# A list scheduler that books VectorE and GpSimd as taking turns, in one step of a hybrid decoder layer

## The chip, the cores and the metric

The kernel runs on one core of a Trainium2 chip. Its engines work side by side, each through its own list of instructions in order: PE (TensorE, matrix products), DVE (VectorE), ACT (ScalarE), POOL (GpSimd), and SP (SyncE), which issues the DMA transfers. A semaphore holds an instruction until what it reads is there. The metric is the device time of one execution in microseconds (us); a smaller number is better.

## What is computed

One inference step of one layer, for 512 new prompt tokens and 8 x 8 sample tokens with stored states: three token mixers beside each other (A is HGRN2, B is mLSTM, C is a gated delta rule, all recurrent over chunks), each branch projected to 1024 channels, merged by gates, one output projection, a LayerNorm, a SwiGLU FFN and a second LayerNorm. Everything is float32.

```python
proj = jnp.einsum('bld,dn->bln', h, w_in[l])          # all inputs of A, B, C and the merge gates
...
a = bc[..., :, None] * jnp.einsum('bhtk,bhsk->bhts', kc, kc) * _masked_exp(strict, diff)
sol = lax.linalg.triangular_solve(eye + a, rhs, left_side=True, lower=True, unit_diagonal=True)
...
z = jnp.einsum('blnc,ncd->blnd', ys, w_branch[l])
gates = jax.nn.sigmoid(mg.reshape(B, L, N_BRANCH, D_MODEL).astype(f32))
merged = jnp.sum(gates * z.astype(f32), axis=2).astype(dt)
h = _layer_norm(ALPHA * h.astype(f32) + (merged @ w_out[l]).astype(f32), ln1_g[l], ln1_b[l]).astype(dt)
gate, up = jnp.split(h @ w_ffn_in[l], 2, axis=-1)
ff = (jax.nn.silu(gate) * up) @ w_ffn_out[l]
h = _layer_norm(ALPHA * h.astype(f32) + ff.astype(f32), ln2_g[l], ln2_b[l]).astype(dt)
```

## The kernel before

Activations lie with channels on the 128 partitions and the 576 tokens in the columns, in two halves of 288. Every large product is made in three passes: `split` (line 524) parts a float32 operand into a rounded high part (a cast on ACT, `wh`, `xh`, `hh`) and a low part (a subtraction on DVE, `wl`, `xl`, `hl`), and `gemm` (line 546) adds high x high, high x low and low x high. So each weight that DMA brings (`load_w`, line 532: raw tile `wr`, then `wh` and `wl`) costs DVE one subtraction of 1024 columns before TensorE can use its low part.

All instructions are first recorded by `Plan` in the order of the program; `Plan.schedule` (line 272) then plays a model of the five engines forward and picks, at each step, the instruction that can start earliest, with ties by priority. The lists that result are the program; because one line of the file issues all of them, every row of the profile bears the number 434. [...] `FLEX` is a string of site letters: an operation recorded with such a letter (`plan.tt`, `plan.ts`, `plan.copy`, `plan.square`) may go to any of several engines, and `place` picks the one on which it is modelled to end first, with POOL's length weighted by `PSLOW`; other sites keep their first engine.

`ORDER` (line 33) is the order in which the stages are recorded: v (projection and convolution of C), p (preparation of a chunk of C), di (the inverse of the 32 x 32 diagonal blocks of C's triangular systems, `gdn_diag`, line 890), m (merging the blocks' inverses, `gdn_merge`, first product `pp`), c (the chunk steps of C, `c_step`, products `ks`, `tv`, `su`, `po`), C (sample heads of C), h (heads of A, products `pz`), a and A (chunk steps and sample heads of A, product `spo`), bq, bv, B, BS (mLSTM, result `bnt`), and X, Y, Z (the 24 merges: a projection `p` of 48 matmuls and a branch product `g` of 24). A + or - raises or lowers the priority from there on. The projections `p` depend on nothing but weights, so they are what fills TensorE while a branch waits.

`gdn_diag` is a chain on DVE: 31 times a product `dp` and an addition to `dY`, each on the result of the one before; the inverse then goes by DMA to DRAM and back into the tile `Tm`, which `pp` reads. `kk` is the product from which the blocks come. In the first LayerNorm (class `LN`, line 1543) each row block `lr` of 128 channels has a mean `m` and a factor `rstd` applied, is split into `hh` and `hl`, and goes into sums `acc`; `T` and `S` are the sums of activation and weight blocks of the FFN's first product, which has seven products `pq` in place of eight (`act_blocks`, line 1690; `weight_blocks`, line 1724). `fg` and `fu` are gate and up part of the FFN, `fh` and `fl` the split of their product.

Of the kernel before, what the change touches and what calls it, by code (L numbers as in the profile page):

```python
# [19 lines left out]
H = 4  # L20
# [11 lines left out]

ORDER = "- v20 v02 v10 + rc rb v31 v21 v32 v30 v11 v01 v00 v22 v12 p1 p2 um p3 p4 cA p0 qe cg di m2 m1 c1 m4 c2 m3 bo cs - c3 c4 C0 aA + h0 h1 h2 C1 C3 h3 a1 a2 bq a3 C2 a4 as A0 co bA A3 A2 ag A1 bv X4 ao br B1 B2 B3 Z3 Z1 B4 Z7 Z0 X0 X1 X6 BS yb ov X3 Z5 Y2 X2 Z6 Y4 X7 Y1 Z2 Y5 X5 Y0 Z4 Y3 Y6 Y7"
WALL = 100000
WDMA = 800
FLEX = "ADEFGacdhioqzIJWMNO"
WARM = 18
# [4 lines left out]
LNEXP = "natural_log_exp_and_others"  # L42
PSLOW = 1.0
LAT = {("DVE", "ACT"): 120.0, ("ACT", "DVE"): 133.0, ("POOL", "ACT"): 72.0, ("POOL", "DVE"): 72.0, ("ACT", "POOL"): 200.0,
       ("DVE", "POOL"): 180.0, ("PE", "ACT"): 215.0, ("PE", "DVE"): 215.0, ("ACT", "PE"): 160.0, ("DVE", "PE"): 145.0,
       ("POOL", "PE"): 95.0, ("PE", "POOL"): 260.0}
PORT = {(1, 3): 0.55, (1, 4): 0.15, (2, 3): 0.8, (2, 4): 0.35}
WINDOW = 3413.0


class _Op:
    __slots__ = ("eng", "fn", "a", "k", "cost", "lat", "nb", "preds", "succs", "prio", "seq",
                 "tiles", "start", "done", "npred", "ready", "alts", "lock", "act")


def _meet(a, b):
    return a[0] < b[1] and b[0] < a[1] and a[2] < b[3] and b[2] < a[3]
# [6 lines left out]
class Plan:  # L64
# [35 lines left out]
    def cost(self, eng, name, out, a, k):  # L100
        n = 1
# [13 lines left out]
        if eng == "ACT":  # L115
            return 95 + 0.834 * n + 93 * cols
        if eng == "DVE":
# [7 lines left out]
        if eng == "POOL":  # L125
            if name == "memset":
                return 66 + 0.79 * n
            if any(0 in [st for st, _ in v.ap[1:]] for v in ap_args):
                return 110 + 1.94 * n
            return (740 if name == "tensor_copy" and n < 100 else 132) + {"tensor_copy": 3.7, "tensor_scalar": 2.86}.get(  # L130
                name, 2.38) * n
        return 450.0
# [16 lines left out]
    def add(self, eng, name, fn, a, k):  # L149
        o = _Op()  # L150
# [9 lines left out]
        preds = set()  # L160
        for t, r in reads:
            preds.update(q for q, w in self.wr.get(t, ()) if _meet(r, w))
        for t, r in writes:
            for book in (self.wr, self.rd):
                lst = book.setdefault(t, [])
                preds.update(q for q, w in lst if _meet(r, w))
                book[t] = [(q, w) for q, w in lst if not _covers(r, w)]
# [13 lines left out]
        if eng == "PE":  # L181
            n = 1
# [5 lines left out]
        if eng == "SP":  # L188
            n = 4
# [7 lines left out]
    def table(self, name, after):  # L197

        o = _Op()
        o.eng, o.fn, o.a, o.k = "ACT", self.nc.scalar.preload_act_table_set, (name,), {}  # L200
        o.seq = len(self.ops)
        o.preds, o.succs, o.prio = {q.seq for q in after}, [], (-1, o.seq)
        o.cost, o.nb, o.tiles, o.alts, o.lock, o.act = 1300.0, 0, [], None, 0, 0.0
        self.ops.append(o)
        return o
# [48 lines left out]
    def schedule(self):  # L254
# [16 lines left out]
        for o in ops:  # L271
            for t in o.tiles:
                if t not in index:
                    g = self.tag[t]
# [32 lines left out]
        end = {}  # L307
        busy = {"DVE": (0.0, 0), "POOL": (0.0, 0)}
        cold, wend, wact, wide = True, 1100.0, 0.0, False
# [29 lines left out]
        while len(order) < len(ops):  # L339
# [37 lines left out]
            if o.eng == "PE":  # L377
# [10 lines left out]
                if cold:  # L388
                    took += act
                part = min(1.0, (wend - s_) / took)  # L390
                wact += act * part
                if part < 1.0:
                    cold = wact < WINDOW * (0.4 if cold else 0.385)
                    wact = act * (1.0 - part)
                    wend += WINDOW
            elif o.eng in busy:
                dve = o.eng == "DVE"
                till, lock = busy["POOL" if dve else "DVE"]
                if o.lock and lock and till > s_:
                    v, g = (o.lock, lock) if dve else (lock, o.lock)  # L400
                    kv = PORT[v, g]
                    kg = 0.33 if v == 1 else 0.2
                    both = min(till - s_, took / (1 - kv)) if dve else min((till - s_) / (1 - kv), took)
                    mine, his = (kv, kg) if dve else (kg, kv)
                    took += mine * both
                    eft["POOL" if dve else "DVE"] += his * both
                    busy["POOL" if dve else "DVE"] = (till + his * both, lock)
                busy[o.eng] = (s_ + took, o.lock)
            eft[o.eng] = s_ + took
# [11 lines left out]
            for u in o.succs:  # L421
                u.npred -= 1
                d = 250.0 if o.eng == "SP" else 0.0 if o.eng == u.eng else LAT.get((o.eng, u.eng), 150.0)
                u.ready = max(u.ready, o.done + d)
                if not u.npred:
                    place(u)
# [20 lines left out]
def tile_hybrid(ctx: ExitStack, tc: tile.TileContext, t):  # L447
# [128 lines left out]
    n = 0  # L576
# [551 lines left out]
    eblA = const.tile([P, 4, 12], F32, name="eblA")  # L1128
    akd, aqe, aatt = [], [], []
    aatt_s = sl([4, 64], name="aatts")  # L1130

    def a_head(h):
# [15 lines left out]
        at = sl([4, P], name="aatt")  # L1148
        aatt.append(at)

# [50 lines left out]
        plan.tt("D", G, q_, b_, q_, ALU.mult)  # L1201
        akd.append(k_)
        aqe.append(q_)

# [808 lines left out]
```

## Time and profile before

Three runs took 1223.35, 1223.98 and 1227.55 us.

| | before |
|---|---|
| median of the runs | 1223.98 us |
| the profiled execution's own time | 1224.88 us |
| its span, from first to last instruction | 1223.1 us |
| mean granted TensorE clock | 0.968 |
| instructions of PE, DVE, ACT, POOL on the page | 8561, 1454, 1055, 390 |

The profile is of one execution. A row of the groups view gives engine, operation, output and inputs by name (numbers left out), shapes, the count, then busy time in us and the mean of one in ns, then the engine's idle time before it and what ended that. A row of the windows view gives a stretch of the span and, for each engine, busy time and count. A row of the timeline gives start and length in us. [...]

### The profile page before, as it was taken

The page shows a single profiled execution, that of the slowest core. Times are in us where ns is not written, and L with a number is a line of the kernel's source. Part 1 is how long each engine was busy: PE and PEld are TensorE (multiplying, and loading weights), DVE is VectorE, ACT ScalarE, POOL GpSimd, SP SyncE. Part 2 cuts the span into 40 slices and gives each one's busy share as a digit, 9 for nine tenths or more (in the row PEclk, how much of TensorE's full clock was granted, in tenths as well). Part 3 has the DMA queues.
Part 4 walks back from the last instruction along what each step waited for, and adds up shares of the span by engine and source line. Part 5 has one row for each costly group of instructions (what it writes and reads, how often), then busy time and mean ns, then how long its engine had stood idle before and what let it go on. Part 6 is the DMA issues. An engine that isn't in the chain of part 4 may idle for free.

```text
span 1223.1 us, 21823 instructions
## 1 busy us (share of the span) xinstructions
PE 1169.0 (96%) x8561; PEld 1132.3 (93%) x8561; DVE 857.7 (70%) x1454; ACT 571.9 (47%) x1055; POOL 403.6 (33%) x390
## 2 busy tenths in 40 slices
PE   9999998999999999899999999959999999999996
PEld 8999987899888989899999999949999999999995
DVE  4789997599775565745644448696999989873237
ACT  6467844345443734543434453553444554432234
POOL 1177623148653553102400004642200024542223
PEclk9999999999998789999999999969999999999998
DMA  8322324311122322223222432222424342533243
GB/s 259 114 100 74 94 70 130 107 52 61 53 87 96 108 91 66 60 97 100 76 82 91 147 89 76 78 70 69 133 89 145 121 157 83 179 112 93 82 115 119
DMA packets 66910, 123.08 MB, mean 101 GB/s; under 512 B 14192, under 2 KB 28272, under 8 KB 66808
## 3 DMA queue, kind: packets, MB, share of 16 engines
q1 hardware_dynamic: 66808, 121.70, 31.3%
q8 instruction: 67, 1.10, 0.4%
q14 instruction: 35, 0.29, 0.1%
HBM read 103.37 MB, written 18.17 MB: 99 GB/s over the span
## 4 chain that ended last, share of the span: by engine, by line
PE 78%; DVE 12%; ACT 4%; issue 2%; DMA 2%; POOL 1%; SPq 0%; DVEq 0%; ACTq 0%; POOLq 0%
PE p L434 25%; PE g L434 21%; PE pq L434 17%; PE tk L434 3%; PE pz L434 2%; DVE wl L434 2%; DVE lr L434 2%; PE os L434 1%; PE spo L434 1%; PE ssu L434 1%; DVE dY L434 1%; DVE dp L434 1%; PE po L434 1%; DVE num L434 1%; DVE z L434 1%
## 5 line engine op out<-in xcount | busy, mean ns | idle before, releaser
L434 DVE TENSOR_TENSOR wl<-wr,wh 128x1024 fp32r<-128x1024 f32 (+3 forms) x172 | 187.7, 1101 | 175.5 <-PE g L434 63.8
L434 ACT CAST wh<-wr 128x1024 fp32r<-128x1024 f32 (+3 forms) x192 | 156.4, 825 | 255.2 <-PE p L434 119.1
L434 PE MATMUL p<-xh,wl 128*128 128x288 f32 x960 | 213.1, 301 | 6.5 <-DVE wl L434 6.5
L434 PE MATMUL p<-xh,wh 128*128 128x288 f32 x960 | 215.3, 302 | 3.0 <-ACT wh L434 2.1
L434 PE MATMUL p<-xl,wh 128*128 128x288 f32 x960 | 213.4, 301 | 0.0
L434 PEld LDWEIGHTS p<-xh,wl 128*128 128x128 f32 x960 | 157.4, 192 | 9.0 <-DVE wl L434 7.2
L434 PEld LDWEIGHTS p<-xh,wh 128*128 128x128 f32 x960 | 157.1, 191 | 5.5 <-ACT wh L434 2.3
L434 PEld LDWEIGHTS p<-xl,wh 128*128 128x128 f32 x960 | 156.9, 191 | 1.5 <-issue 1.1
L434 PE MATMUL g<-fh,wl 128*128 128x320 f32 (+1 forms) x352 | 82.6, 295 | 0.0
L434 PE MATMUL g<-fl,wh 128*128 128x320 f32 (+1 forms) x352 | 82.3, 295 | 0.0
L434 PE MATMUL g<-fh,wh 128*128 128x320 f32 (+1 forms) x352 | 82.3, 294 | 0.0
L434 PE MATMUL pq<-hh,wh 128*128 128x288 f32 x240 | 72.5, 302 | 8.2 <-ACT hh L434 4.1
L434 PE MATMUL pq<-hh,wl 128*128 128x288 f32 x240 | 71.7, 299 | 4.1 <-DVE wl L434 4.1
L434 PE MATMUL pq<-hl,wh 128*128 128x288 f32 x240 | 71.6, 299 | 0.6 <-DVE hl L434 0.6
L434 PE MATMUL pq<-Th,wh 128*128 128x288 f32 x240 | 70.5, 295 | 0.0
L434 PE MATMUL pq<-Tl,wh 128*128 128x288 f32 x240 | 70.5, 294 | 0.0
L434 PEld LDWEIGHTS g<-fh,wl 128*128 128x128 f32 x352 | 57.1, 188 | 0.1
L434 PEld LDWEIGHTS g<-fh,wh 128*128 128x128 f32 x352 | 57.1, 188 | 0.1
L434 PEld LDWEIGHTS g<-fl,wh 128*128 128x128 f32 x352 | 57.0, 188 | 0.0
L434 PEld LDWEIGHTS pq<-hh,wh 128*128 128x128 f32 x240 | 45.8, 191 | 9.8 <-ACT hh L434 4.5
L434 POOL TENSOR_SCALAR acc<-lr 128x288 f32<-128x288 f32 (+2 forms) x4 | 4.9, 1230 | 142.2 <-DVE lr L434 142.2
L434 PEld LDWEIGHTS pq<-hh,wl 128*128 128x128 f32 x240 | 45.9, 191 | 4.3 <-DVE wl L434 4.3
(461 smaller groups left out, 3060.9 us busy)
## 6 DMA issues: line engine op xcount, KB each, us to landing
wr<-wft SPq DMA_DIRECT2D x60, 512.0 KB, 3.5
wr<-wfi SPq DMA_DIRECT2D x20, 512.0 KB, 3.6
wq<-wfi SPq DMA_DIRECT2D x40, 256.0 KB, 3.2
wr<-wfo SPq DMA_DIRECT2D x20, 512.0 KB, 3.5
wr<-wbr SPq DMA_DIRECT2D x24, 256.0 KB, 2.6
fd<-fg SPq DMA_DIRECT2D x20, 288.0 KB, 2.3
fx<-fd SPq DMA_DIRECT2D x20, 288.0 KB, 4.0
wr<-wfo SPq DMA_DIRECT2D x10, 384.0 KB, 3.1
```

Source lines behind the costliest of these rows:

```text
L434: o.fn(*o.a, **o.k)
```

## The change

The table `PORT` goes. In its place an operation with a lock waits, in the model, until the other engine's locked operation has ended (less a lag). Costs of POOL's operations are set anew, a delay is booked between two operations of one engine where the second reads the first's result, and the cold clock multiplies a matmul's length. `PSLOW` goes from 1 to 3, `FLEX` opens other sites (among them m, i, j, n, M, A, C, and no longer a to e or z), and `ORDER` is a new one. The last hunks only index three lists by the head, since the heads are now recorded in the order 2, 0, 3, 1.

```diff
-ORDER = "- v20 v02 v10 + rc rb v31 v21 v32 v30 v11 v01 v00 v22 v12 p1 p2 um p3 p4 cA p0 qe cg di m2 m1 c1 m4 c2 m3 bo cs - c3 c4 C0 aA + h0 h1 h2 C1 C3 h3 a1 a2 bq a3 C2 a4 as A0 co bA A3 A2 ag A1 bv X4 ao br B1 B2 B3 Z3 Z1 B4 Z7 Z0 X0 X1 X6 BS yb ov X3 Z5 Y2 X2 Z6 Y4 X7 Y1 Z2 Y5 X5 Y0 Z4 Y3 Y6 Y7"
+ORDER = "- cA rc v31 v20 v11 v30 + v01 v22 um rb v21 v00 v10 v02 v32 v12 p3 p1 p4 p2 p0 qe di m1 m2 c1 aA cs c2 m3 c3 m4 c4 cg C0 - + bo h2 ov C1 h0 bA h3 C3 h1 bq a1 a2 a3 C2 a4 co br as A0 A3 ag A2 A1 bv ao B1 Z1 Z0 B2 X6 X0 Z3 Z5 B3 B4 X3 BS X1 Z7 X7 yb Y2 Y5 Y0 X5 X2 Z6 Y3 X4 Z2 Y4 Y1 Z4 Y6 Y7"
...
-FLEX = "ADEFGacdhioqzIJWMNO"
+FLEX = "DWNOgCnhwjtpqsGmrFBoMAfxidK"
...
-PSLOW = 1.0
+PSLOW = 3.0
 LAT = {("DVE", "ACT"): 120.0, ("ACT", "DVE"): 133.0, ("POOL", "ACT"): 72.0, ("POOL", "DVE"): 72.0, ("ACT", "POOL"): 200.0,
        ("DVE", "POOL"): 180.0, ("PE", "ACT"): 215.0, ("PE", "DVE"): 215.0, ("ACT", "PE"): 160.0, ("DVE", "PE"): 145.0,
-       ("POOL", "PE"): 95.0, ("PE", "POOL"): 260.0}
-PORT = {(1, 3): 0.55, (1, 4): 0.15, (2, 3): 0.8, (2, 4): 0.35}
+       ("POOL", "PE"): 95.0, ("PE", "POOL"): 260.0, ("PE", "PE"): 0.0, ("DVE", "DVE"): 121.0,
+       ("ACT", "ACT"): 131.0, ("POOL", "POOL"): 40.0}
...
-            return 95 + 0.834 * n + 93 * cols
+            return (70 if isinstance(k.get("bias"), bass.AP) else 95) + 0.834 * n + 93 * cols
...
-                return 66 + 0.79 * n
+                return 60 + 0.72 * n
+            if name == "tensor_copy":
+                return 148 + 0.8 * n if n < 100 else 120 + 3.36 * n
+            if name == "tensor_scalar":
+                return 120 + 2.6 * n
             if any(0 in [st for st, _ in v.ap[1:]] for v in ap_args):
-                return 110 + 1.94 * n
-            return (740 if name == "tensor_copy" and n < 100 else 132) + {"tensor_copy": 3.7, "tensor_scalar": 2.86}.get(
-                name, 2.38) * n
+                return 126 + 1.76 * n
+            return 146 + 2.16 * n
...
+        o.raw = set(preds)
...
-        busy = {"DVE": (0.0, 0), "POOL": (0.0, 0)}
+        held = {"DVE": 0.0, "POOL": 0.0}
...
                 if cold:
-                    took += act
+                    took *= 1.92 if o.act < 0 else 1.82
...
-            elif o.eng in busy:
-                dve = o.eng == "DVE"
-                till, lock = busy["POOL" if dve else "DVE"]
-                if o.lock and lock and till > s_:
-                    v, g = (o.lock, lock) if dve else (lock, o.lock)
-                    kv = PORT[v, g]
-                    kg = 0.33 if v == 1 else 0.2
-                    both = min(till - s_, took / (1 - kv)) if dve else min((till - s_) / (1 - kv), took)
-                    mine, his = (kv, kg) if dve else (kg, kv)
-                    took += mine * both
-                    eft["POOL" if dve else "DVE"] += his * both
-                    busy["POOL" if dve else "DVE"] = (till + his * both, lock)
-                busy[o.eng] = (s_ + took, o.lock)
+            elif o.lock:
+                other, lag = ("POOL", 99.0) if o.eng == "DVE" else ("DVE", 43.0)
+                took += max(0.0, held[other] - lag - s_)
+                held[o.eng] = s_ + took
+                if o.fn.__name__ == "tensor_scalar" and o.eng == "POOL":
+                    held[o.eng] -= max(0.0, 0.71 * o.cost - 105.0)
...
-                d = 250.0 if o.eng == "SP" else 0.0 if o.eng == u.eng else LAT.get((o.eng, u.eng), 150.0)
+                d = LAT.get((o.eng, u.eng), 250.0 if o.eng == "SP" else 150.0)
+                if o.eng == u.eng != "SP" and o.seq not in u.raw:
+                    d = 0.0
...
-    akd, aqe, aatt = [], [], []
+    akd, aqe, aatt = [None] * H, [None] * H, [None] * H
...
-        aatt.append(at)
+        aatt[h] = at
...
-        akd.append(k_)
-        aqe.append(q_)
+        akd[h] = k_
+        aqe[h] = q_
```

The instructions are the same work on other engines and in another order: DVE has 1648 in place of 1456, POOL 205 in place of 395, ACT 1037 in place of 1039; PE has 8011 and SP 376 as before. Three places:

DVE in the chain of `dp` and `dY` (dX and dY are the blocks and their inverses, `wl` a weight's low part, `so` a decayed state of a sample head, `ge` a gate), before:

```order
L434 TENSOR_TENSOR dp_467<-dX_450,dY_451 64x256
L434 TENSOR_TENSOR dY_451<-dY_451,dp_467 64x16x16
L434 TENSOR_TENSOR dp_468<-dX_450,dY_451 64x255
L434 TENSOR_TENSOR dY_451<-dY_451,dp_468 64x15x17
L434 TENSOR_TENSOR wl_555<-wr_553,wh_554 128x1024
L434 TENSOR_TENSOR dp_469<-dX_450,dY_451 64x252
L434 TENSOR_TENSOR dY_451<-dY_451,dp_469 64x14x18
L434 TENSOR_TENSOR dp_470<-dX_450,dY_451 64x247
L434 TENSOR_TENSOR dY_451<-dY_451,dp_470 64x13x19
L434 TENSOR_TENSOR dp_471<-dX_450,dY_451 64x240
L434 TENSOR_TENSOR dY_451<-dY_451,dp_471 64x12x20
L434 TENSOR_TENSOR dp_472<-dX_450,dY_451 64x231
```

and at the same products with the change:

```order
L434 TENSOR_TENSOR dp_434<-dX_422,dY_423 64x231
L434 COPY dX_455<-dY_456 32x8x8
L434 TENSOR_TENSOR dY_423<-dY_423,dp_434 64x21x11
L434 TENSOR_TENSOR dp_435<-dX_422,dY_423 64x240
L434 TENSOR_TENSOR so_574<-ss_563,eblC 128x512
L434 TENSOR_TENSOR wl_577<-wr_575,wh_576 128x1024
L434 TENSOR_TENSOR dY_423<-dY_423,dp_435 64x20x12
L434 TENSOR_TENSOR wl_583<-wr_581,wh_582 128x1024
L434 TENSOR_TENSOR dp_436<-dX_422,dY_423 64x247
L434 TENSOR_SCALAR ge_559<-ge_559 128x576
L434 TENSOR_TENSOR dY_423<-dY_423,dp_436 64x19x13
```

The chain's steps now have weight splits, a gate and the decay of sample states between them more often; the decays were POOL's.

POOL in the first LayerNorm (`lr` are the row blocks, `acc` the running sums, `T` the sums of activation blocks, `S` and `wq` those of weights), before:

```order
L434 TENSOR_TENSOR acc_1267_1376<-acc_1267_1376,lr_1467 128x288
L434 TENSOR_TENSOR acc_1268_1377<-acc_1268_1377,lsq_1494 128x288
L434 TENSOR_TENSOR acc_1268_1377<-acc_1268_1377,lsq_1496 128x288
L434 TENSOR_TENSOR acc_1267_1376<-acc_1267_1376,lr_1476 128x288
L434 TENSOR_TENSOR acc_1268_1377<-acc_1268_1377,lsq_1498 128x288
L434 TENSOR_TENSOR S_1479_1588<-wq_1582,wq_1584 128x512
L434 TENSOR_TENSOR wq_1584<-wq_1584,wq_1585 128x512
L434 TENSOR_TENSOR S_1500_1609<-wr_1605,wr_1606 128x512
L434 TENSOR_TENSOR lr_1423<-lr_1423,rstd_1379 128x288
L434 TENSOR_TENSOR lr_1441<-lr_1441,rstd_1379 128x288
L434 TENSOR_TENSOR lr_1476<-lr_1476,rstd_1379 128x288
L434 TENSOR_TENSOR lr_1476<-lr_1476,m_1271_1380 128x288
```

and with the change:

```order
L434 TENSOR_TENSOR acc_1267_1376<-acc_1267_1376,lr_1458 128x288
L434 TENSOR_TENSOR hl_1394<-lr_1467,hh_1386 128x288
L434 TENSOR_TENSOR acc_1267_1376<-acc_1267_1376,lr_1467 128x288
L434 TENSOR_TENSOR acc_1267_1376<-acc_1267_1376,lr_1476 128x288
L434 TENSOR_TENSOR lr_1448<-lr_1448,rstd_1379 128x288
L434 TENSOR_TENSOR lr_1476<-lr_1476,rstd_1379 128x288
L434 TENSOR_TENSOR lr_1476<-lr_1476,m_1271_1380 128x288
L434 TENSOR_TENSOR hl_1395<-lr_1476,hh_1387 128x288
L434 TENSOR_TENSOR T_1440_1549<-lr_1476,lr_1441 128x288
L434 TENSOR_TENSOR T_1428_1537<-lr_1458,lr_1423 128x288
L434 TENSOR_TENSOR T_1434_1543<-lr_1467,lr_1434 128x288
L434 TENSOR_TENSOR T_1446_1555<-lr_1485,lr_1448 128x288
```

The sums of squares (`lsq`) and weight blocks have gone to DVE, and of the row blocks some; two splits (`hl`) have come.

PE in the steps of the gated delta rule (`qp`, `qt`, `pp` belong to the merging, `su`, `po`, `ks` to a step, `ssu` to a sample head, `p` is a projection; x4 stands for four such rows in succession), before:

```order
L434 MATMUL qp_536<-pm_535,Tm_533 64x64 x4
L434 MATMUL p_602<-xh_98,wh_600 128x288
L434 MATMUL p_602<-xl_106,wh_600 128x288 x2
L434 MATMUL p_602<-xh_98,wl_601 128x288 x2
L434 MATMUL qt_537<-Tm_533,pm_535 128x128 x3
L434 MATMUL ssu_590<-vm_589,kh_419 128x512
L434 MATMUL ssu_590<-vm_589,kl_420 128x512
L434 MATMUL qt_537<-Tm_533,pm_535 128x128
L434 MATMUL p_602<-xh_99,wh_600 128x288
L434 MATMUL ssu_593<-vm_592,kh_419 128x512
L434 MATMUL ssu_593<-vm_592,kl_420 128x512
L434 MATMUL p_602<-xh_99,wh_600 128x288
```

and with the change:

```order
L434 MATMUL po_516<-cqkv_226,Sc_499 128x128
L434 MATMUL po_516<-catt_376,vn_513 128x128
L434 MATMUL po_516<-cqkv_254,Sc_499 128x128
L434 MATMUL po_516<-catt_376,vn_513 128x128
L434 MATMUL pp_523<-Tm_517,nAT_395 64x64 x3
L434 MATMUL ks_527<-Sc_515,cqkv_268 128x128
L434 MATMUL ks_527<-Sc_515,cqkv_240 128x128
L434 MATMUL ks_527<-Sc_515,cqkv_313 128x128
L434 MATMUL ks_527<-Sc_515,cqkv_212 128x128
L434 MATMUL po_532<-cqkv_327,Sc_515 128x128
L434 MATMUL qt_525<-Tm_518,pm_524 64x64 x4
L434 MATMUL p_602<-xh_99,wl_601 128x288
```

The projections between the steps' own products have become fewer, and the sample head's products are gone from here.

More of the change, by code (lines that the diff above doesn't have):

```diff
@@ L52 @@
     __slots__ = ("eng", "fn", "a", "k", "cost", "lat", "nb", "preds", "succs", "prio", "seq",
-                 "tiles", "start", "done", "npred", "ready", "alts", "lock", "act")
+                 "tiles", "start", "done", "npred", "ready", "alts", "lock", "act", "raw")
 def _meet(a, b):
@@ L203, in table @@
         o.cost, o.nb, o.tiles, o.alts, o.lock, o.act = 1300.0, 0, [], None, 0, 0.0
+        o.raw = set()
         self.ops.append(o)
```

## The prediction

> **What bounds the kernel now.** I read the page first (busy shares, then the chain that ended last), then the windows view stage by stage, then the waits of TensorE.
>
> ```profile
> span 1223.1 us, 21823 instructions
> ...
> PE 1169.0 (96%) x8561; PEld 1132.3 (93%) x8561; DVE 857.7 (70%) x1454; ACT 571.9 (47%) x1055; POOL 403.6 (33%) x390
> ...
> PE 78%; DVE 12%; ACT 4%; issue 2%; DMA 2%; POOL 1%; SPq 0%; DVEq 0%; ACTq 0%; POOLq 0%
> ```
>
> TensorE is busy for 96% of the span and makes 78% of the chain; the change gives it no matmul less. What can be won is the time in which TensorE stands or crawls, and 96% hides the crawling: a slow matmul is busy too. So I count records against the rate of an undisturbed stage. In the table below the columns are the stretch, its length, the busy time and records of PE, weight loads, DVE, ACT and POOL, the granted clock, DMA share and GB/s.
>
> ```profile
> 0.00:50.00 50.00, 45.21 (x299) 43.05 (x300) 30.60 (x81) 28.46 (x73) 4.61 (x29) 0.97 0.66 215
> 160.20:206.70 46.50, 38.95 (x268) 37.40 (x267) 41.81 (x104) 16.35 (x23) 16.36 (x10) 0.93 0.30 78
> 207.00:247.00 40.00, 39.80 (x335) 35.47 (x335) 19.48 (x43) 16.11 (x36) 6.59 (x8) 1.00 0.42 133
> 250.00:375.00 125.00, 122.38 (x911) 113.91 (x911) 103.83 (x170) 57.17 (x91) 75.15 (x73) 0.99 0.18 60
> 375.00:450.00 75.00, 73.63 (x446) 65.71 (x445) 41.64 (x62) 40.92 (x94) 34.28 (x36) 0.82 0.34 111
> 391.00:411.00 20.00, 20.00 (x73) 16.63 (x73) 7.90 (x11) 10.29 (x21) 10.08 (x7) 0.50 0.29 108
> 475.00:600.00 125.00, 118.53 (x883) 115.58 (x882) 81.70 (x153) 59.79 (x139) 33.65 (x39) 0.99 0.25 79
> 600.00:775.00 175.00, 175.00 (x1320) 174.67 (x1319) 85.67 (x124) 74.07 (x114) 20.62 (x21) 1.00 0.29 91
> 776.60:851.40 74.80, 59.12 (x362) 54.48 (x362) 62.25 (x92) 38.77 (x76) 37.78 (x34) 0.84 0.23 75
> 850.00:1000.00 150.00, 149.99 (x1135) 149.73 (x1134) 139.28 (x255) 70.59 (x126) 11.73 (x7) 1.00 0.41 135
> 1000.00:1070.00 70.00, 67.01 (x500) 66.07 (x500) 64.27 (x91) 34.95 (x59) 34.61 (x22) 1.00 0.39 121
> 1200.00:1224.00 24.00, 10.97 (x85) 10.03 (x83) 17.66 (x32) 10.93 (x22) 8.62 (x9) 0.79 0.33 114
> ```
>
> The full rate is 175.00 / 1320 = 0.1326 us a record. A stage's loss is its length less its records at that rate: 74.8 - 48.0 = 26.8 us in the first LayerNorm (776.6 to 851.4), 46.5 - 35.5 = 11 in the diagonal blocks of the gated-delta branch (160.2 to 206.7), 15.9 in the HGRN2 sample heads (375 to 450; there matmuls differ in shape, so this is an upper end), 7.9 in the mLSTM stages, 10.4 at the start, 4.2 in the HGRN2 heads, 3.7 in 1000 to 1070, 12.7 in the tail. In all some 93 us; the FFN and the merges lose nothing.
>
> Next, what the change is about: whether VectorE and GpSimd block each other. A stretch of the first LayerNorm, start, length, engine, operation; DVE, then POOL:
>
> ```profile
> 843.28 0.46 DVE L434 TENSOR_TENSOR T<-lr,T 128x288 f32<-128x288 f32 x1
> 843.78 1.57 DVE L434 TENSOR_TENSOR T<-T,lr 128x288 f32<-128x288 f32 x1
> 846.76 1.69 DVE L434 TENSOR_TENSOR T<-lr 128x288 f32<-128x288 f32 x1
> 843.38 1.65 POOL L434 TENSOR_TENSOR Tl<-T,Th 128x576 fp32r<-128x576 f32 x1 [2.82 <-DVE S3l L434]
> 846.09 2.04 POOL L434 TENSOR_TENSOR Tl<-T,Th 128x576 fp32r<-128x576 f32 x1 [1.06 <-DVE Tl L434]
> ```
>
> The 288-wide DVE operation takes 0.46 us alone, and 1.57 and 1.69 where POOL had begun first. It ends 0.32 us behind POOL's end both times (845.35 against 845.03, 848.45 against 848.13). They take turns, as the new planner books; the old table let both go on at reduced speed.
>
> **The first LayerNorm, taken at -8.** By the order of instructions, between its first statistics and its last operand split DVE has 92 instructions before (as in the trace) and 110 after, POOL 34 and 15. What moves is mostly the LayerNorm's own row arithmetic (second excerpt above): 13 of 288 columns, 3 of 512, 2 of 576. The prices, DVE and POOL for the same work:
>
> ```profile
> L434 DVE TENSOR_TENSOR us<-us,pq 128x288 f32<-128x288 f32 x40 | 17.9, 446 | 0.8 <-PE pq L434 0.6
> L434 DVE TENSOR_TENSOR kwl<-kw,kwh 128x512 fp32r<-128x512 f32 x16 | 10.4, 685 | 0.0
> L434 DVE TENSOR_TENSOR fg<-fg,fu 128x576 f32<-128x576 f32 x11 | 8.3, 752 | 0.0
> L434 POOL TENSOR_TENSOR acc<-acc,lr 128x288 f32<-128x288 f32 x12 | 10.9, 904 | 7.5 <-DVE lr L434 7.3
> L434 POOL TENSOR_TENSOR lr<-lr,rstd 128x288 f32<-128x288 f32 x7 | 7.9, 1139 | 8.6 <-ACT rstd L434 8.6
> L434 POOL TENSOR_TENSOR fg<-fg,fu 128x576 f32<-128x576 f32 x9 | 16.8, 1871 | 45.8 <-ACT wh L434 25.7 <-DVE fu L434 11.6 <-ACT fg L434 8.6
> ```
>
> DVE's work without waits is 55 x 0.446 + 31 x 0.685 + 6 x 0.752 = 50.3 us before; its recorded 62.25 thus holds 12 of waiting for POOL. After: 68 x 0.446 + 34 x 0.685 + 8 x 0.752 = 59.6. The two engines together, if every microsecond is a turn, go from 50.3 + 37.8 = 88 to 59.6 + 15 x 1.11 (37.78 / 34) = 76, a gain of 12; since 88 is more than the 74.8 it ran in, part of it did run side by side, and 12 is the upper end. At the other end DVE alone counts: 62.25 before, 59.6 plus 15/34 of the 12 us of waiting, 64.9, after: 3 us slower. DVE stands idle for 12.5 of the 74.8 us, waiting on a chain of rows, and on that chain a step falls from 1.139 to 0.446; so I lean to the turns and take -8.
> [...]
>
> **The diagonal blocks, -8.** Here one engine runs 31 dependent steps (dp, then dY) while TensorE lives on projection matmuls whose weight splits (wl) must pass the same engine.
>
> ```profile
> 169.35 0.29 DVE L434 TENSOR_TENSOR dp<-dX,dY 64x135 f32<-64x135 f32 x1
> 169.68 1.02 DVE L434 TENSOR_TENSOR dY<-dY,dp 64x135 f32<-64x135 f32 x1
> 170.63 0.80 DVE L434 SCALAR_TENSOR_TENSOR gate<-gate,par,gx 128x576 f32<-128x576 f32 x1
> 174.90 1.21 DVE L434 TENSOR_TENSOR wl<-wr,wh 128x1024 fp32r<-128x1024 f32 x1
> 169.46 1.09 POOL L434 TENSOR_TENSOR so<-ss,eblC 128x512 f32<-128x512 f32 x1 [2.90 <-DVE dY L434]
> 176.16 0.85 PE L434 MATMUL p<-xh,wl 128*128 128x288 f32 x2 [2.24 <-DVE wl L434]
> 195.57 0.53 PE L434 MATMUL p<-xh,wl 128*128 128x288 f32 x2 [3.51 <-DVE wl L434]
> 166.80:197.90 31.10, 11.45 (x50) 8.58 (x50) 3.63 (x3) 0.92 0.20 64
> ```
>
> The last row counts wl alone in that chain: 3 splits, 3.63 us on DVE. TensorE waits for them (2.24 and 3.51) and the clock falls (0.92 to 0.93). By the order, 6 splits stand in the chain afterwards, and 357 projection matmuls instead of 238 between the last kk product and the first pp. Added to the chain: three splits, 3.6; two so, 2 x 0.685 = 1.4; about one gate and one ge more, 1.3; small mask work, some 2; together 8. So the stage is 46.5 + 8 = 54.5 long, and its matmuls need 35.5 + 119 x 0.1326 = 51.3: a loss of 3.2 in place of 11. POOL's so made a 0.29 step last 1.02; that goes, but I leave it in reserve. Ends: -11 if all is filled, 0 if the chain grows by 16, for instance because a split moved in needs weights that land late.
>
> **The gated-delta steps, +5.5.** The fillers are taken from behind: in the stretch of 207 to 247 the order shows 62 projection matmuls before and 26 after, and the sample head C0's six matmuls have gone ahead. The steps are a chain of small products and evacuations; if that sets the length, TensorE idles for the 36 x 0.1326 = 4.8 us taken out, and 0.7 for C0. Ends: 0, if TensorE (39.8 of 40 busy) was the bound; far above, if the clock falls (the slower rival).
>
> **HGRN2 heads, samples, mLSTM.** In the heads DVE and POOL hold 104 and 75 of 125 us; z products of POOL (0.8 to 1.3 us each) become DVE's at half that; half of the 4.2 lost comes back, -2 (ends -4 and 0). The sample heads are spaced: their products stand at places 2334, 2410, 2500, 2505 of TensorE's list, where three stood within 14 places (2354 to 2367), and the stretch of 20 us at clock 0.50 with 73 records sits there. At the full rate 73 records need about 10; I take -4 of that (ends -10 and 0). The mLSTM steps get 15 more projection and 24 more branch matmuls as cover:
>
> ```profile
> PE bnt L434 <- DVE num L434: 4.7, 4, 2.1
> ```
>
> The 4.7 us in four waits is what the cover can hide, out of 7.9 lost: -4 (ends -8 and 0). Start and tail: -1 (ends -2 and 0).
>
> **FFN, 0.** Elementwise products and low parts (fg, fl) go to DVE: in 1000 to 1070 DVE has 91 instructions of 64.27/91 = 0.706 us and POOL 22; in 850 to 1000, where POOL has 7, DVE's mean is 139.28/255 = 0.546. All 113 on DVE at 0.546 is 62 us, in 70. What hides it is TensorE's stream of products; if that cover went (DVE is at 93% in 850 to 1000), each would cost its 0.75.
>
> **Sum.** -8 - 8 + 5.5 - 2 - 4 - 4 - 1 = -21.5. The profiled execution took 1224.88 us (span 1223.1 and 1.8 around it), 0.9 above the median of 1223.98, within the three runs' spread. 1224.9 - 21.5 = 1203.4, say 1203.
>
> **Rivals.** A measurement of this kernel can tell about 0.5%, 6.1 us, from no change: faster is below 1217.9, slower above 1230.1.
> *More of the holes close*: the good ends are -12, -11, 0, -4, -10, -8, -2, together -47: 1178. For it: all these stages lose by waiting, not by work. Against: six ends at once. 0.15.
> *VectorE takes the bound over*: it gains nearly 200 instructions (1456 to 1648 in the order), POOL loses 190 (395 to 205), so the change surely acts, but it may only swap turns for work. First LayerNorm +3, diagonal 0, steps +5.5, and the -11 of the other terms as they are: 1224.9 - 2.5 = 1222.4. For it: DVE at 83% in the LayerNorm and the heads. Against: its waiting there goes with POOL's work. 0.19.
> *The gated-delta steps fall to half clock*, the slower one. The 299 records left in that stretch at 39.8/335 = 0.119 us are 35.5 us. What the half clock costs shows behind the wait at 195.57:
>
> ```profile
> 196.87 0.68 PE L434 MATMUL p<-xh,wh 128*128 128x288 f32 x2
> 197.34 0.68 PE L434 MATMUL p<-xl,wh 128*128 128x288 f32 x2
> ```
>
> Two matmuls begin each 0.47 us, 0.235 for one against 0.1326, 1.8 times as much; so the stretch grows by 0.8 x 35.5 = 28. With the 5.5 that is 33.5, against 27 won elsewhere: 1224.9 + 6.5 = 1231. It decides from a loss of 27 us in that stretch. For it: a busy TensorE did run at 0.50 in 391 to 411 with thin products; against: this stretch held 1.00 with the same products. 0.11.
> [...]
>
> **How the numbers follow.** The forecast, with its terms off by a third to a half each way, covers 1190 to 1217 and has 0.55. Range over all cases: 1180 to 1226, which takes in half of the good rival and most of the unchanged one, leaving about 2 in 10 outside. Faster: 0.55 + 0.15 + 0.04 of the third case = 0.74. Within 0.5%: 0.15 of the third and 0.03 of the slower = 0.18. Slower: 0.08.
>
> **What would show it.** The LayerNorm's stretch from first m to last Tl near 67 us, its clock above 0.84, DVE rows of lr and T near 0.45: the first term; 75 with DVE above 90% busy: the second rival. First pp about 54 us behind the last kk with waits for wl below 2 us: the second term. First pp to last po near 40 us at clock 1.00: the third; at 0.50, the slower rival. The four waits of bnt below 2 us in all, no 20 us stretch at 0.50 around the sample heads. I am wrong if the loss stays near 93 us with new names: TensorE waiting for wl, hl or f on a VectorE that never stands.

## The result, and the profile after

The changed kernel takes 1172.33 us (1169.57 to 1173.14, four runs) against 1225.14 (1223.35 to 1227.55): a ratio of 0.9564, 95% interval 0.9539 to 0.9588. That is 53 us faster; 21.5 were forecast, and 1172 lies below the range. The direction was right; the forecast gain was less than half of the measured one. The profiled execution took 1172.4 us. From the page:

```profile
span 1170.6 us, 21690 instructions
...
PE 1142.4 (98%) x8561; PEld 1113.2 (95%) x8561; DVE 856.4 (73%) x1646; ACT 574.0 (49%) x1053; POOL 157.6 (13%) x200
...
PE 84%; DVE 10%; ACT 3%; DMA 1%; issue 1%; SPq 0%; DVEq 0%; ACTq 0%
```

DVE has 192 instructions more, and is busy for no longer (856.4 us after 857.7): what it gained in work it lost in waiting for POOL. If each row of DVE is set against the shortest tenth of the rows of the same operation and shape, its rows were stretched by 124 us in all before and by 46 after.

The windows of the changed kernel, at the same stages as in the prediction (stretch, length, busy time and records of PE, weight loads, DVE, ACT, POOL, granted clock as a share of full speed, DMA share, GB/s):

```profile
0.00:50.00 50.00, 47.43 (x336) 45.71 (x337) 36.26 (x97) 28.09 (x69) 6.61 (x33) 1.00 0.70 228
140.80:194.70 53.90, 53.07 (x394) 50.98 (x392) 46.67 (x126) 28.66 (x42) 1.54 (x4) 1.00 0.35 96
194.70:225.70 31.00, 31.00 (x280) 28.61 (x280) 13.47 (x34) 8.63 (x21) 0.41 (x2) 1.00 0.35 110
243.00:343.20 100.20, 100.09 (x752) 92.94 (x752) 92.61 (x199) 50.55 (x79) 15.87 (x16) 1.00 0.21 63
343.20:428.40 85.20, 83.49 (x589) 76.37 (x588) 54.23 (x91) 45.77 (x99) 11.14 (x21) 0.96 0.36 109
458.90:546.00 87.10, 85.72 (x648) 83.58 (x649) 52.44 (x115) 35.58 (x84) 19.93 (x30) 1.00 0.28 87
740.00:801.50 61.50, 51.80 (x343) 49.17 (x342) 60.12 (x110) 37.29 (x75) 14.89 (x15) 0.89 0.29 89
801.50:1015.70 214.20, 214.20 (x1623) 214.20 (x1623) 191.00 (x357) 104.65 (x183) 4.63 (x3) 1.00 0.40 129
```

Losses by the prediction's count, length less records at 0.1326 us:

| stage | before | after | difference | forecast |
|---|---|---|---|---|
| start (0 to 50) | 10.4 | 5.4 | -5.0 | -1 (with the tail) |
| diagonal blocks (140.8 to 194.7) | 11.0 | 1.7 | -9.3 | -8 |
| gated-delta steps (194.7 to 225.7) | -4.4 | -6.1 | -1.7 | +5.5 |
| HGRN2 heads (243.0 to 343.2) | 4.2 | 0.5 | -3.7 | -2 |
| HGRN2 samples (343.2 to 428.4) | 15.9 | 7.1 | -8.8 | -4 |
| mLSTM (458.9 to 546.0) | 7.9 | 1.2 | -6.7 | -4 |
| first LayerNorm (740.0 to 801.5) | 26.8 | 16.0 | -10.8 | -8 |
| FFN's products (801.5 to 1015.7; before 850 to 1070) | 3.2 | -1.0 | -4.2 | 0 |

They sum to -50.2 of the 52.5 by which the profiled executions differ. (The steps' small products are quicker than 0.1326, 31.00 us for 280 records or 0.111 each after the change, hence the negative losses there; only the difference counts.) The half clock went with the holes: outside the tail the granted clock was 0.50 for 68 us before and 20 after. The waits of TensorE (in all, times, longest):

```profile
PE os L434 <- DVE cl L434: 4.4, 1, 4.4
...
PE bnt L434 <- DVE num L434: 1.7, 3, 0.6
PE pq L434 <- DVE wl L434: 1.1, 1, 1.1
```

The waits of p for wl, 6.5 us before, are gone, those of bnt are 1.7 in place of 4.7, and the longest left stands in the first LayerNorm.

### The profile page after: what moved, and what is told of

Read it like the earlier page. It is cut to its first block, busy times and chain, and to the rows that moved or that the text cites. A ratio compares the mean times of both kernels' runs of the same rounds, so it can differ in the third digit from the quotient of the medians.

```text
span 1170.6 us, 21690 instructions
## 1 busy us (share of the span) xinstructions
PE 1142.4 (98%) x8561; PEld 1113.2 (95%) x8561; DVE 856.4 (73%) x1646; ACT 574.0 (49%) x1053; POOL 157.6 (13%) x200
## 4 chain that ended last, share of the span: by engine, by line
PE 84%; DVE 10%; ACT 3%; DMA 1%; issue 1%; SPq 0%; DVEq 0%; ACTq 0%
PE p L434 27%; PE g L434 22%; PE pq L434 19%; PE tk L434 3%; PE pz L434 2%; DVE lr L434 2%; PE os L434 1%; PE po L434 1%; PE ssu L434 1%; DVE wl L434 1%; PE spo L434 1%; DVE num L434 1%; ACT wh L434 1%; PE su L434 1%; PE pp L434 1%
## 5 line engine op out<-in xcount | busy, mean ns | idle before, releaser
L434 DVE TENSOR_TENSOR wl<-wr,wh 128x1024 fp32r<-128x1024 f32 (+3 forms) x172 | 167.9, 986 | 164.1 <-PE g L434 72.0
L434 PE MATMUL p<-xh,wh 128*128 128x288 f32 x960 | 211.9, 299 | 0.0
L434 POOL TENSOR_TENSOR mrg<-mrg,msg 128x576 f32<-128x576 f32 x16 | 24.6, 1536 | 185.2 <-DVE msg L434 171.2
L434 PE MATMUL pq<-Th,wL 128*128 128x288 f32 x160 | 47.1, 294 | 0.0
```

Of the source, the lines that this page charges most:

```text
L434: o.fn(*o.a, **o.k)
```

## The experiments

The change has three parts that can be had apart: the engines (FLEX and PSLOW), the booking (turns, costs, delays between dependent operations) and the stage order. Ratios are against the kernel before in the same session, with 95% intervals.

### Parts undone and parts alone

Old engines and old order, so that only the booking is new:

```diff
 (the changed kernel)
+ORDER, FLEX, PSLOW as before
```

> The new booking alone: turns, POOL's new costs, the delays between dependent operations of one engine; stage order, open sites and POOL's weight as before, so POOL keeps about 395 instructions. Booking theory (the lists were bad because the planner did not see the waits): most of the 53 us comes, 1172 to 1190. Engine theory (POOL's work on VectorE is what pays) and order theory (the new stage order pays): 1212 to 1226, VectorE's rows still stretched by POOL's.

Measured: 1228.27 us, 1.0056 (1.0031 to 1.0080). No gain; the booking theory falls. DVE's stretched rows are up, at 146 us.

New order and booking, old engines:

```diff
 (the changed kernel)
+FLEX = "ADEFGacdhioqzIJWMNO"
+PSLOW = 1.0
```

> New booking and new stage order, with the old open sites and POOL's weight; POOL keeps about 400 instructions. Engine theory: 1205 to 1225, first LayerNorm's hole still near 27 us. Order theory: 1175 to 1190, the holes of the mixers closed, the LayerNorm's left.

Measured: 1228.01 us, 1.0042 (1.0023 to 1.0060). The order theory falls: on the old engines neither the booking alone nor booking and order together bring anything. (The new order alone was not run.)

New engines alone:

```diff
 (the kernel before)
+FLEX = "DWNOgCnhwjtpqsGmrFBoMAfxidK"
+PSLOW = 3.0
```

> Only the open sites and POOL's weight are new; booking and stage order are old. If moving POOL's work to VectorE pays by itself (fewer turns on the chip, whatever the planner believes): 1195 to 1210, near the 1199 of the kernel with the old booking alone. If it pays only with lists planned on the new booking: 1212 to 1226, the holes of the diagonal blocks and the first LayerNorm still above 10 and 22 us.

Measured: 1218.26 us, 0.9922 (0.9892 to 0.9951), as the second expectation has it: lists planned on the old booking keep most of their holes, although DVE's stretched rows are down to 49 us. That the turns go is not enough by itself.

New engines and order, old booking:

```diff
 (the kernel before)
+ORDER, FLEX, PSLOW as changed; akd, aqe, aatt by head
```

> New stage order, open sites and POOL's weight, planned with the old booking (shared speed, old costs). Booking theory: the gain is lost, 1205 to 1225. Engine theory and order theory: it stays, 1170 to 1188.

Measured: 1199.34 us, 0.9813 (0.9791 to 0.9834), between the two expectations. More than half of the gain hangs on the booking (0.0187 of 0.0436 is left), again with DVE's stretched rows at 46 us.

New engines and booking, old order:

```diff
 (the changed kernel)
+ORDER as before
```

> New booking, open sites and POOL's weight, with the old stage order; POOL falls to about 190 instructions. Engine theory: 1172 to 1190, VectorE's stretched rows gone, first LayerNorm's hole near 17 us as in the changed kernel. Order theory: 1205 to 1225, with the first LayerNorm (which the order string does not touch) alone better by 10.

Measured: 1183.43 us, 0.9677 (0.9656 to 0.9698), as the engine theory has it. The order is worth the rest, about 0.011. So the engines come first, and the booking pays only on top of them. On the old order, too, the booking is worth 0.0245 (0.9922 to 0.9677).

Only POOL's weight undone:

```diff
 (the changed kernel)
-PSLOW = 3.0
+PSLOW = 1.0
```

> The changed kernel with POOL's weight at 1 in place of 3: the same sites open, but POOL takes some 370 operations again. If the weight is what keeps turns away: 1205 to 1230, VectorE's stretched rows back near 120 us. If the choice of open sites does: 1172 to 1190.

Measured: 1214.81 us, 0.9917 (0.9893 to 0.9941). Its page:

```profile
PE 1163.8 (96%) x8561; PEld 1129.1 (93%) x8561; DVE 860.9 (71%) x1474; ACT 568.9 (47%) x1040; POOL 399.6 (33%) x385
```

POOL is back at 400 us, and DVE's stretched rows at 141. The choice of engine (`place`) compares free times and lengths and does not ask about turns; the weight is what keeps POOL out.

### What the turns cost on the chip

The kernel before with its own lists; POOL's arithmetic issued on DVE where it stood:

```diff
             for o in self.schedule():
+                if o.eng == "POOL" and o.fn.__name__ in ("tensor_tensor", "tensor_scalar"):
+                    o.fn = getattr(self.nc.vector, o.fn.__name__)
                 o.fn(*o.a, **o.k)
```

> The kernel before, its lists as they were planned, but POOL's tensor_tensor and tensor_scalar operations issued on VectorE at the same place of the program (some 300; POOL keeps copies and memsets). No replanning. If turns on the chip are the loss and their going is the gain: 1195 to 1215, VectorE's stretched rows (124 us) gone. If the planning is the gain: 1220 to 1245, since VectorE carries all of it in lists made for two engines.

Measured: 1203.27 us, 0.9837 (0.9791 to 0.9883), 20 us with no new plan at all (and better than the new engines planned on the old booking, 0.9922). DVE's stretched rows fall from 124 us to 12. Its page, its windows of the diagonal blocks and the first LayerNorm, and two groups of DVE:

```profile
PE 1157.3 (97%) x8561; PEld 1124.5 (94%) x8561; DVE 874.4 (73%) x1736; ACT 572.8 (48%) x1055; POOL 33.6 (3%) x108
```

```profile
156.60:203.10 46.50, 40.19 (x268) 38.62 (x268) 42.04 (x112) 16.55 (x23) 0.49 (x2) 0.89 0.29 79
763.60:832.40 68.80, 56.29 (x361) 53.00 (x360) 58.56 (x126) 38.15 (x75) 0.00 (x0) 0.88 0.26 86
```

```profile
L436 DVE TENSOR_TENSOR lr<-lr,m 128x288 f32<-128x288 f32 x16 | 7.0, 453 | 0.1
L436 DVE TENSOR_TENSOR lr<-lr,rstd 128x288 f32<-128x288 f32 x16 | 7.0, 453 | 0.0
```

POOL's 403.6 - 33.6 = 370 us of arithmetic cost DVE 874.4 - 857.7 = 17 us of busy time, since 124 - 12 = 112 us of stretched rows went with it. The lr rows of DVE took 743 and 706 ns in the kernel before, and 453 here:

```profile
L434 DVE TENSOR_TENSOR lr<-lr,rstd 128x288 f32<-128x288 f32 x9 | 6.4, 706 | 0.0
L434 DVE TENSOR_TENSOR lr<-lr,m 128x288 f32<-128x288 f32 x8 | 5.9, 743 | 0.2
```

The first LayerNorm's loss falls from 26.8 to 68.8 - 361 x 0.1326 = 20.9, but the diagonal stretch stays 46.5 long with 268 records, as before: taking the turns away does not close that hole.

The same edit on the changed kernel:

```diff
 (the changed kernel, same two lines in issue)
```

> The changed kernel, its lists as planned, with what is left of POOL's tensor_tensor and tensor_scalar operations (some 90) issued on VectorE at the same place. If the turns that are left (46 us of stretched VectorE rows) still cost: 1160 to 1169. If they lie where nothing waits, VectorE only gets more work: 1172 to 1182.

Measured: 1169.75 us, 0.9555 (0.9535 to 0.9576), not to be told from the changed kernel's 0.9564, and between the two expectations. The turns that are left cost nothing that shows. Planned anew without POOL, the arithmetic is no better:

```diff
     def add(self, eng, name, fn, a, k):
+        if eng == "POOL" and name in ("tensor_tensor", "tensor_scalar"):
+            eng, fn = "DVE", getattr(self.nc.vector, name)
...
+            if o is not None and rec is self.G:
+                continue
```

> The changed planner, with no tensor_tensor or tensor_scalar offered to POOL, planned anew. If lists made for one engine are better than lists in which single operations change engine: below the kernel that moves them in place, 1158 to 1168. If the stage order fits only the lists it came with: 1170 to 1185.

Measured: 1177.29 us, 0.9613 (0.9588 to 0.9638), as the second expectation has it. No version here beats the changed kernel clearly.

### Which part of the booking

Turns booked at shared speed again (by the old table `PORT`, in which a DVE and a POOL operation that overlap slow each other in the model), all else as changed:

```diff
-                other, lag = ("POOL", 99.0) if o.eng == "DVE" else ("DVE", 43.0)
-                took += max(0.0, held[other] - lag - s_)
...
+                kv = PORT[v, g]
+                kg = 0.33 if v == 1 else 0.2
...
```

> The changed kernel, with the old table of shared speed in place of turns; delays and costs stay new. If the turns are what the booking adds: 1190 to 1200, VectorE's stretched rows up again from 46 us. If the delay is: 1172 to 1180.

Measured: 1180.95 us, 0.9616 (0.9579 to 0.9653): about 6 us by the ratios (9 against the control below, which ran in the same session), and 6 sit in the first LayerNorm, whose loss goes from 16.0 to 22.3. This is no more than the planner without POOL lost by its new plan, so it is not clearly the turns.

No delay between dependent operations of one engine:

```diff
-("PE", "PE"): 0.0, ("DVE", "DVE"): 121.0, ("ACT", "ACT"): 131.0, ("POOL", "POOL"): 40.0}
+("PE", "PE"): 0.0, ("DVE", "DVE"): 0.0, ("ACT", "ACT"): 0.0, ("POOL", "POOL"): 0.0}
```

> The changed kernel, without the booked delay between two dependent operations of one engine (121, 131 and 40 ns set to 0); turns and costs stay booked. If what the booking adds beyond the choice of engines is this delay (POOL being nearly idle, few turns are left to book): 1190 to 1200. If it is the turns: 1172 to 1180.

Measured: 1202.42 us, 0.9787 (0.9742 to 0.9832): 27 us lost by the ratios (31 against the same control), more than the first expectation had. The larger part of the booking is this delay, not the turns that the change is named after. POOL's new costs and the new factor for the cold clock were not taken back alone.

The delay for DVE alone:

```diff
-("ACT", "ACT"): 131.0, ("POOL", "POOL"): 40.0}
+("ACT", "ACT"): 0.0, ("POOL", "POOL"): 0.0}
```

> The changed kernel, with the delay booked for VectorE alone (ScalarE's and POOL's set to 0). If VectorE's chains are what was booked too short: 1170 to 1180. If ScalarE's chains are: 1190 to 1203, as without any delay.

Measured: 1189.03 us, 0.9708 (0.9667 to 0.9748): between the two. DVE's delay counts, and so does what was left out here, ScalarE's and POOL's together.

The delay for dp and dY alone:

```diff
+            d1.dly = d2.dly = True
...
-                if o.eng == u.eng != "SP" and o.seq not in u.raw:
+                if o.eng == u.eng != "SP" and (o.seq not in u.raw or not u.dly):
                     d = 0.0
```

> The changed kernel, with the delay between dependent operations of one engine booked only for the dp and dY of the diagonal blocks, and nowhere else. If the delay works by its place (a chain booked too short leaves the weight splits too late in VectorE's list): the diagonal hole falls from 11.9 us (no delay at all) to 2 to 5, the first LayerNorm's stays near 22, and the time is 1188 to 1196. If it works by a general shift of the lists: the diagonal hole stays above 8 and the time above 1197.

Measured: 1190.0 us, 0.9721 (0.9681 to 0.9761): from one chain 8 us by the ratios, 12 by the times, which are of two sessions. That is as much as all of DVE's delays together gave (0.9708, same session as this). The diagonal stretch without any delay, then with the delay there, each followed by wl alone within the chain of dp and dY:

```profile
146.60:191.50 44.90, 37.11 (x261) 36.30 (x262) 38.14 (x109) 16.59 (x25) 2.86 (x3) 0.92 0.34 87
154.50:184.90 30.40, 11.09 (x48) 8.05 (x46) 3.66 (x3) 0.93 0.25 65
```

```profile
144.10:200.40 56.30, 54.41 (x401) 52.05 (x400) 49.13 (x130) 29.35 (x43) 2.10 (x5) 1.00 0.34 97
152.00:191.90 39.90, 18.79 (x86) 13.47 (x84) 7.30 (x6) 1.00 0.26 82
```

Three splits become six, 261 records 401, the loss falls from 10.3 to 3.1 and the clock holds. TensorE's waits in the first of the two:

```profile
163.85 0.85 PE L434 MATMUL p<-xh,wl 128*128 128x288 f32 x2 [2.88 <-DVE wl L434]
183.93 0.85 PE L434 MATMUL p<-xh,wl 128*128 128x288 f32 x2 [4.70 <-DVE wl L434]
```

This is the picture of the kernel before (2.24 and 3.51 for the same tile). What the delay is can be read in the trace of before, in the chain and among independent operations:

```profile
190.26 0.38 DVE L434 TENSOR_TENSOR dY<-dY,dp 64x220 f32<-64x220 f32 x1
190.67 0.37 DVE L434 TENSOR_TENSOR dp<-dX,dY 64x207 f32<-64x207 f32 x1
848.38 0.45 DVE L434 TENSOR_TENSOR T<-lr,lr 128x288 f32<-128x288 f32 x1
848.74 0.45 DVE L434 TENSOR_TENSOR T<-lr,T 128x288 f32<-128x288 f32 x1
```

The dependent one begins 0.03 us behind its predecessor's end, the independent one 0.09 before it: 0.12 us apart, and 62 such links make 7.4 us. Read so, a planner that books none believes the chain done that much earlier, and sets in DVE's list only the splits that fit the short chain; on the chip the splits behind them come late, as the waits of 2.88 and 4.70 show.

A control, three figures moved by 3 or 4 ns:

```diff
-("PE", "DVE"): 215.0 ... ("DVE", "DVE"): 121.0 ... other, lag = ("POOL", 99.0)
+("PE", "DVE"): 219.0 ... ("DVE", "DVE"): 124.0 ... other, lag = ("POOL", 102.0)
```

> The changed kernel with three planner figures moved by 3 or 4 ns (219 for 215, 124 for 121, 102 for 99): a control for how much the lists' luck is worth, since the planner takes other decisions after any small change. Either theory: the median stays within 6 us of 1172; if it moves by 10 us or more, differences of that size between planner variants prove nothing.

Measured: 1171.7 us, 0.9535 (0.9491 to 0.9578). The one nudge tried moved nothing that shows, so the 27 us of the delay are not likely to be luck of the lists; for the steps of 6 and 8 us one nudge is a thin control.

### The gated-delta steps

The kernel before, 36 fillers left out of the stretch:

```diff
+                if first < i < last and names[i].startswith("p_") and out and not (o.k["start"] or o.k["stop"]):
+                    out -= 1
+                    continue
                 o.fn(*o.a, **o.k)
```

> The kernel before, its lists as planned, with 36 projection matmuls left out between the first pp and the last ks of the gated-delta steps (the outputs of those projections lack these products). If the steps' own chain sets the length there, as the prediction had it, the stretch stays near 39.4 us, TensorE stands for some 5 of it, and the time stays within 1 us of before. If TensorE was the bound, the stretch falls by 36 x 0.1326 = 4.8, to about 34.6, and so does the time.

Measured: 1223.74 us, 1.0015 (0.9988 to 1.0043). The stretch:

```profile
202.90:240.40 37.50, 34.23 (x295) 30.05 (x294) 18.63 (x40) 16.03 (x36) 6.04 (x8) 1.00 0.44 142
```

From first pp to last ks it was 39.4 us. It shrinks by 1.9 of 4.8, and TensorE stands for the rest: the mechanism of the forecast's +5.5 exists in these lists, at a little over half its size. The time does not follow the 1.9 (1.0015). Then all foreign work put off behind the last ks:

```diff
+            late = [i for i in range(first + 1, last) if i not in keep]
...
+            seq = [i for i in range(last + 1) if i not in gone] + late + list(range(last + 1, len(order)))
```

> The kernel before, its lists as planned, but between the first pp and the last ks everything that the gated-delta steps do not need (projection matmuls and their splits, the sample head, gates, on all engines) is issued behind the last ks instead. If foreign work in the lists of VectorE and ScalarE is what kept the stretch at 37.5 us after the fillers were left out: it falls to 29 to 32, as in the changed kernel (31.0). If the steps' own chain takes that long: it stays at 35 to 38. The time: within 6 us of before either way, since the work is only put off.

Measured: 1237.03 us, 1.0139 (1.0100 to 1.0178), slower than the 6 us expected either way; from 206 to 250, which takes in the first 10 us behind the stretch, TensorE is busy for 37.06 of 44.00 us at clock 0.90. The stretch itself comes out as the second expectation has it. Here it is whole, then up to the last pp, then behind it:

```profile
203.50:239.70 36.20, 32.74 (x282) 29.71 (x281) 11.70 (x29) 8.53 (x26) 1.05 (x1) 0.95 0.24 72
203.50:230.70 27.20, 25.40 (x232) 22.70 (x230) 9.76 (x24) 6.68 (x19) 1.05 (x1) 1.00 0.32 95
230.70:239.70 9.00, 7.34 (x50) 7.01 (x51) 1.94 (x6) 1.85 (x7) 0.00 (x0) 0.81 0.00 0
```

The theory of foreign work falls: with 282 records, nearly all its own, the stretch takes 36.2 us (at clock 0.95, so some 1.8 us of it are the slow clock), where the changed kernel takes 31.0 for 280. The order of the steps' own products differs: here the last merging product (pp) ends 9 us before the last ks, and the tail of the chain runs bare; in the changed kernel pp goes on to 1.1 us before it (224.6 of 225.7), and TensorE is busy for 31.00 of 31.00. The kernel with the old order, new engines and new booking has an early last pp too, 7.8 us before the last ks, and projection matmuls in the tail (the whole stretch, then the tail):

```profile
197.50:232.40 34.90, 33.85 (x306) 31.30 (x306) 14.59 (x33) 13.62 (x31) 1.64 (x5) 1.00 0.38 121
224.60:232.40 7.80, 7.80 (x68) 7.48 (x67) 5.21 (x11) 4.44 (x9) 0.82 (x1) 1.00 0.46 159
```

Its count, 34.9 - 306 x 0.1326 = -5.7, is nearly the changed kernel's -6.1. So late merges cover the tail and projections cover it as well. This is read from the traces; no kernel moved either alone.

## Why the prediction was wrong

*The bound* was right: TensorE's holes by count, and 93 us of them to be had.

*The turns* were right as a mechanism: moving POOL's arithmetic in place takes DVE's stretched rows from 124 us to 12 and brings 20 us. That this is near the forecast's 21.5 is chance: of the forecast only the LayerNorm's and the heads' terms, -10 together, rested on POOL's arithmetic going to DVE, and in place the LayerNorm gains 5.9 and the diagonal stretch nothing.

**The step that failed is the sum.** It gave the booked delay between dependent operations of one engine, which stands in the diff, no term, and took the lists as otherwise worth the same. The delay is worth 27 us on top of the new engines and order. In the sum's own terms the stages came to -50.2 for -21.5, and the largest misses are the gated-delta steps (-1.7 for +5.5), the samples (-8.8 for -4), the FFN (-4.2 for 0) and the start (-5.0 for -1, of which some 3.5 is chance, see below). The diagonal blocks held part of the delay unseen, since their -8 was read from lists that the delay had shaped: planned without it that stretch loses 10.3, with it 1.7. In the first LayerNorm it is 21.9 without and 16.0 with it. Where the rest of the 27 us lies was not traced.

*First LayerNorm*, -8 forecast, -10.8 measured. The row arithmetic moved to DVE, as said, gives 26.8 to 20.9 in place; the rest comes with the lists, and needs both parts of the booking. With shared-speed turns the same stretch loses 69.4 - 355 x 0.1326 = 22.3, and without the delay 68.8 - 354 x 0.1326 = 21.9:

```profile
741.10:810.50 69.40, 55.23 (x355) 51.53 (x353) 59.34 (x112) 37.58 (x75) 13.98 (x14) 0.85 0.26 82
764.00:832.80 68.80, 55.47 (x354) 51.94 (x352) 60.36 (x112) 38.27 (x75) 13.53 (x14) 0.88 0.25 80
```

*Diagonal blocks*, -8 forecast, -9.3 measured, and for the reason given: first pp 53.9 us behind the last kk (54.5 forecast), six splits, no wait for wl. But it was booked to what the order shows, with nothing said of why the planner put the splits there. The hole closes where new engines and new booking meet, whatever the order. The same stretch with the old order, then with the old booking, then with the new booking alone:

```profile
143.90:197.50 53.60, 51.81 (x380) 49.12 (x377) 47.36 (x124) 30.04 (x43) 0.99 (x2) 1.00 0.41 108
145.90:191.90 46.00, 38.69 (x260) 37.53 (x260) 40.49 (x112) 16.14 (x24) 1.55 (x2) 0.89 0.35 93
154.30:202.70 48.40, 35.15 (x264) 33.57 (x262) 41.52 (x107) 16.72 (x24) 13.79 (x9) 0.91 0.35 97
```

By the count they lose 3.2, 11.5 and 13.4.

*Gated-delta steps*, +5.5 forecast, -1.7 measured: the term with the wrong sign. It held the chain's length fixed at before's and took only the fillers away. In before's lists that costs TensorE 4.8 - 1.9 = 2.9 us; the new lists have their own products in the gaps.

*Samples and mLSTM*, -8 forecast, -15.5 measured: sized at half of what was lost. What the prediction named did go: the 20 us at clock 0.50 but for 7, and 3 of the 4.7 us that bnt waited. But the new order, which spaces the sample heads, is not the whole cause. The stretch around them, before and after, then with the old order, then with the old engines:

```profile
340.00:460.00 120.00, 116.82 (x768) 106.83 (x767) 76.32 (x113) 57.90 (x118) 59.81 (x65) 0.87 0.29 96
340.00:460.00 120.00, 117.75 (x860) 109.79 (x860) 82.21 (x143) 66.06 (x148) 19.47 (x31) 0.97 0.32 98
340.00:460.00 120.00, 119.80 (x847) 111.30 (x847) 72.01 (x124) 56.65 (x116) 23.96 (x34) 0.93 0.32 101
340.00:460.00 120.00, 111.50 (x742) 99.70 (x742) 68.73 (x113) 53.94 (x117) 61.97 (x66) 0.90 0.28 87
```

Counted as 1.00 or 0.50, these clocks are some 31, 7, 17 and 24 us at half speed. Two kernels with before's lists there (36 fillers left out; foreign work put off) had 0.89 and 0.90 from 340 to 460, some 25 us, so with the old engines little of the gain is left, and with the old order part of it.

*Start*, -1 against -5: most of the difference is no effect of the change. The kernel with the 36 fillers left out has before's lists in the first 50 us, and lost 50.0 - 325 x 0.1326 = 6.9 there, at clock 1.00, where the profile of before lost 10.4 at 0.97:

```profile
0.00:50.00 50.00, 46.11 (x325) 43.99 (x326) 32.26 (x83) 30.06 (x76) 6.47 (x32) 1.00 0.65 215
```

Against that the changed kernel's 5.4 is 1.5 better. Turns have little room in it either: in the first 50 us POOL is busy for 4.61 us before and 6.61 after, with memsets and a few copies alone.

*FFN*, 0 against -4.2: the count showed a loss of 3.7 in 1000 to 1070, and the text then called the stage covered. Moving POOL's arithmetic in place takes that loss away, so it hung on POOL's share of the work (the same 70 us of the FFN there):

```profile
982.40:1052.40 70.00, 70.00 (x531) 70.00 (x530) 65.48 (x117) 39.74 (x64) 0.00 (x0) 1.00 0.43 137
```

*The rivals*. "More of the holes close", 1178 at 0.15, is nearest to what came. It still went 6 us too little far: FFN, start and steps went past the ends it took for them (0, -2 and 0). VectorE did not become the bound. The half clock in the steps, the slower rival, did not come with the change, but it came with the booking on the old engines:

```profile
202.70:250.90 48.20, 47.40 (x328) 42.44 (x328) 16.10 (x35) 13.99 (x34) 11.31 (x11) 0.77 0.28 84
```

48.2 us for 328 records at clock 0.77, about 9 us more than before for as many records.

What stays open: the parts do not add (in place 20, delay 27, turns booked 6, order 14, of 53), since each plan is a new one; how much of the order's share is the order itself and how much its fit to this booking; and what POOL's new costs and the cold-clock factor do alone.

## What to carry to other kernels

Where two engines take turns, ask what the weaker one saves: here 370 us of POOL's arithmetic cost VectorE only 17 us, because its rows, stretched by 124 us before, were then stretched by 12. In these runs a list planned without the links of 0.12 us set the weight splits behind the chain of dp and dY too late: TensorE stood for 2.88 and 4.70 us, and the stretch ran at clock 0.92, where it had 1.00 with these links booked. So measure the link between dependent operations and book it before tuning an order. And when a diff holds several figures of a planner, give each a term, the quiet ones too.

## What the runs showed of the hardware

In the trace of before a dependent VectorE operation (dp after dY, at 190.67) started 0.03 us after its predecessor's end and an independent one (T, at 848.74) 0.09 us before it, 0.12 us apart. VectorE's busy time in that trace holds waiting for GpSimd: with GpSimd's arithmetic moved in place, 282 more instructions raised it by 17 us, and the stretched rows fell from 124 us to 12.

In the kernel with the booking alone TensorE was busy and stayed at half clock for some 19 us. It waited 12 us for a DMA at the head of the gated-delta steps, and then (the wait; two stretches behind it):

```profile
202.70 1.01 PE L434 MATMUL pp<-Tm,nAT 128*128 128x128 f32 x3 [11.95 <-DMA Tm<-td]
202.70:212.00 9.30, 8.63 (x46) 7.65 (x46) 1.47 (x3) 0.95 (x2) 0.00 (x0) 0.50 0.22 63
212.00:222.00 10.00, 9.87 (x47) 7.73 (x46) 2.54 (x4) 4.12 (x8) 3.29 (x2) 0.50 0.16 52
```

Busy by the profile for 18.5 of 19.3 us, it ran at 0.50 throughout.
